# Another order for the first mixer: value projection, gates, state-space output and a half-and-half last projection

## The chip, the cores and the metric

The kernel runs on one core of one Trainium2 chip. Its time is the device time of one execution in microseconds (us); lower is better. The kernel before was timed in three executions. A fourth was recorded by the hardware profiler, and all rows below come from that one.

## The reference, cut to what matters

The program runs two blocks one after the other on a sequence of 256 tokens of width 1024, all in 32-bit floats. The first block is an adaptive-norm hybrid mixer followed by a mixture of 32 experts; the second block has its own mixer and experts and is not touched here. This is the part that the change is about (the linear recurrences are cut to their names):

```python
c_act = silu(c)
mod = (c_act @ ada_w + ada_b)                       # 6 vectors of 1024
sh1, sc1, g1, sh2, sc2, g2 = split(mod, 6)
h = rmsnorm(x, norm1_g) * (1 + sc1) + sh1
x = x + g1 * hybrid_mixer(h)
h = rmsnorm(x, norm2_g) * (1 + sc2) + sh2
x = x + g2 * moe_ffn(h)                             # top 4 of 32 experts

def hybrid_mixer(h):
    proj = h @ w_in                                 # 1024 x 6672: q,k,v | z | b,a | ssd_z | xbc | dt
    qkv = silu(causal_dwconv(gdn_qkv, w))           # convolution over 4 tokens
    q, k = l2norm(...), l2norm(...)                 # 8 heads of 128
    o = gated_delta_rule_chunked(q, k, v, beta, g)  # per chunk of 64 tokens a triangular
                                                    # inverse, then 4 chunks in sequence
    o = rmsnorm(o) * silu(z)
    xbc = silu(causal_dwconv(xbc, w) + b)
    y = ssd_chunked(...) * silu(ssd_z)              # state-space part, 16 heads of 64
    y = rmsnorm(y)
    return concatenate([o, y]) @ w_out              # 2048 x 1024
```

## The kernel before, in words

Weights come from memory in chunks of 1 MB (256 columns of 1024 rows, or 128 rows of 2048 columns of `ada_w`). All chunks, those of the experts too, go through one list that SP works off in order (`Stream`, line 173 issues each load). A load is issued when its slot is free: four slots while the mixer runs, six more ("ring 1") when the mixer has given back one side of its memory, and five at the mixer's end. So the next stage's loads queue up behind this stage's.

A projection is done in split precision: each weight chunk is turned into a high part `wh` (by ACT, line 296) and a rest `wl` (by DVE or POOL, line 293), one chunk ahead of its use, and `mm3` makes three matrix products of each pair (high by high, high by rest, rest by high). A chunk has two halves of 24 matmuls of 128x256 each; "half-chunk" below means these 24. All matmuls are issued at line 283, all plain ACT operations at line 296, all two-operand DVE operations at line 293.

The work of the first mixer is written as generators. `weave(main, (fill, rate))` takes one step of `main`, then `rate` steps of `fill`, and so on; a scheduler then places the instructions on their engines. `chain` runs generators one behind the other, `turns` in turns, `run_all` to the end. The stages, with the times of the profiled execution:

- **Stage A, 35 to 198 us.** Projection of `xbc` (6 chunks), `k` and `q` (8 chunks), each followed by `conv_silu`: ACT makes `cv_y`, DVE adds three shifted products (line 661), ACT takes a tanh (`cv_t`), DVE joins them to silu (line 664; silu(y) is y/2 times 1 + tanh(y/2), so the weights carry a factor 0.5). Beside it the state-space part `ssd()`, and the second third of the adaptive vector (`ada_batch(1)`): eight sums of 128x2048 on DVE (lines 477 and 479), then small matmuls.
- **Preparation, 198 to 291 us.** `gdn_prep`: decay matrices `dS`, `dT`, the products of keys, the triangular inverse by doubling. As fill at rate `FILL1` = 0.8: the state-space gate (4 chunks), then the values `v` (4 chunks) in turns with `ssd_cat`, which lays the gated state-space output out for the last projection. `ada_batch(2)` runs beside it at rate 0.25.
- **Recurrence, 291 to 363 us.** `gdn_steps`: four chunks of 64 tokens in sequence, each with two groups of heads; chunks 0 and 1 make token half 0 of `o`, chunks 2 and 3 half 1. As fill at rate `FILL2` = 0.6: the gate `z` (4 chunks), then `ssd_out` (the state-space half of the last projection, 4 chunks); what is left of the fill is run after it.
- **Tail, 363 to 411 us.** Ring 1 is opened; `o` is transposed (line 1126), multiplied by the gate and split; the other half of the last projection (4 chunks, both token halves) runs in split precision; behind each chunk `router_logits` adds the result to `x`, transposes it (line 1202) and multiplies it by the router weights.
- **Routing, 411 to 440 us.** The logits (line 1219), the choice of experts and their rows. The experts' biases `bsrc` (line 1627) are loaded by SP behind the 15 expert chunks. Then the experts run, 440 to 1340 us.

Of the kernel before, what the change touches and what calls it, by code (L numbers as in the profile page):

```python
# [24 lines left out]
KD = 8  # L25
# [92 lines left out]
class Stream:  # L118
# [57 lines left out]
    def get(self, split=False):  # L176
# [7 lines left out]
        return v  # L184

# [68 lines left out]
def chain(*gens):  # L254
    for g in gens:
        yield from g
# [13 lines left out]
def kernel_body(ctx, tc, ins, consts, out):  # L270
# [192 lines left out]
    def ada_batch(b):  # L463
# [4 lines left out]
        SP.dma_start(g, ada_b[0:1, 2048 * b + g0:2048 * b + g0 + 1024].to_broadcast([P, 1024]))  # L468
        acc = None
# [20 lines left out]
        ws.give(slot)  # L490

# [53 lines left out]
    nc.vector.tensor_scalar(col_w, pb[:, :144], 0.5, None, op0=ALU.mult)  # L545
    hb = pA.tile([P, 12], F32, name="hb")
    nc.vector.tensor_scalar(hb, colv("ssd_conv_b"), 0.5, None, op0=ALU.mult)
# [39 lines left out]
def mixer1(k):  # L587
# [4 lines left out]
    hT, h32, ro, col_w, hb, colv = k.hT, k.h32, k.ro, k.col_w, k.hb, k.colv  # L592
# [59 lines left out]
    def conv_silu(pj, wc, ct, nct, dst, bias=None):  # L652
# [44 lines left out]
    def twice_silu(pj):  # L697

        th = pA.tile([P, 512], F32, tag="t2a", bufs=2, name="hs")
        act(th, pj, AF.Tanh, scale=0.5)  # L700
        V.scalar_tensor_tensor(th, th, 1.0, pj, op0=ALU.add, op1=ALU.mult)
        return th

# [8 lines left out]
    def emit(c, pj):  # L712
        if c < 8:
            xT = pA.tile([P, T], F32, tag="vT", bufs=2, name="xT")
            conv_silu(pj, cws, c, 12, xT, bias=hb[:, c:c + 1])
# [4 lines left out]
        else:  # L720
            conv_silu(pj, cws, c, 12, bc[:, c - 8], bias=hb[:, c:c + 1])
# [236 lines left out]
    def ssd_gate():  # L958
        def emit(i, pj):
            g2 = twice_silu(pj)  # L960
# [8 lines left out]

        rsy = pA.tile([P, 4], F32, name="rsy")  # L970
        k.rstd(rsy, ssy, 0.25 / 512, pA, "rsy")
        for t in range(2):
            for g in range(2):
                y = ys[t][:, g * 512:(g + 1) * 512]
                V.tensor_scalar(y, y, rsy[:, t * 2 + g:t * 2 + g + 1], 0.5, op0=ALU.mult, op1=ALU.mult)
# [16 lines left out]
    def out_part(i, pj):  # L992
        sl = slice(i * 256, (i + 1) * 256)
        d = pA.tile([P, 2, 256], F32, tag="t2a", bufs=2, name="d")
# [18 lines left out]
    ada2 = k.ada_batch(2)  # L1013
# [5 lines left out]
    S = a4("S")  # L1019
    o = [a4(f"o{t}") for t in range(2)]  # L1020
# [12 lines left out]
    def gdn_steps():  # L1033
        for n in range(4):
# [33 lines left out]
            for hg in range(2):  # L1068
# [18 lines left out]
                if c == 1:  # L1087
                    gdn_norm(t, hg)
                yield
# [3 lines left out]
    def emit_z(i, pj):  # L1093
        if not zs:
            zs.extend(a4(f"zs{i}").rearrange("p (c s) -> p c s", c=4) for i in range(2))
        g2 = pA.tile([P, 512], F32, tag="zt", bufs=1, name="zt")
# [1451 lines left out]
```

## Time and profile before

| | us |
|---|---|
| three timed executions | 2166.81, 2175.94, 2178.86 |
| their median | 2175.94 |
| the profiled execution | 2167.87 |
| its span, first to last instruction | 2166.1 |
| of that, up to the end of the tail | 411 |
| routing | 411 to 440 |
| first experts | 440 to 1340 |
| second block | 1340 to 2166 |

PE is busy for 1929.7 us of the span (89%), DVE for 696.2 and ACT for 437.5. A share of the whole span says little here, since the stages differ: the first experts stand at the limit of the memory, while the first mixer has PE, DVE and ACT busy together. So the stretches of the mixer are to be read one by one. A busy PE is not a PE at its peak: its records lengthen when it waits for weights or runs at the lower of its two clock levels, and the granted clock stands beside each stretch.

### The profile page before, as it was taken

The numbers are of one execution on the slowest core, as the hardware profiler recorded it, in microseconds if no ns is written. First come the engines' busy times: TensorE is split into PE (matmuls) and PEld (weight loads), VectorE is DVE, ScalarE is ACT, GpSimd is POOL, SyncE is SP. The second block draws the span as 40 slices with busy tenths as digits, with TensorE's granted clock in tenths as the row PEclk, the third lists the DMA queues.
The fourth block names the chain that finished last, engine by engine and source line by source line (L and its number), as shares of the span: only waits on it lengthen the run. The fifth ranks groups of instructions, "written<-read, shape, count | busy, mean of one in ns | idle before, by whom it ended". The sixth has DMA issues, their size and how long they took to land. (4 is left out here: it accounts for less than half of the span.)

```text
span 2166.1 us, 27479 instructions
## 1 busy us (share of the span) xinstructions
PE 1929.7 (89%) x11276; PEld 1017.1 (47%) x11277; DVE 696.2 (32%) x1436; ACT 437.5 (20%) x1030; POOL 256.8 (12%) x206
## 2 busy tenths in 40 slices
PE   6889899589999999999999999889999688878777
PEld 3878788533343434334343433387779332212111
DVE  4888847421111211111111011464755200000001
ACT  3555434221010100001010100143443210101001
POOL 2524312100000000000000000243433000000000
PEclk8989889789999999999999999999999799999999
DMA  8553425679999999999999999925238699999997
GB/s 311 200 190 118 157 80 184 256 312 419 420 420 421 413 421 421 402 421 420 418 421 385 422 421 421 328 84 180 74 104 334 247 421 421 420 420 421 421 421 282
DMA packets 170747, 706.67 MB, mean 326 GB/s; under 512 B 20775, under 2 KB 83796, under 8 KB 95860
## 3 DMA queue, kind: packets, MB, share of 16 engines
q1 hardware_dynamic: 170612, 704.80, 82.0%
q8 instruction: 93, 1.52, 0.3%
q14 instruction: 42, 0.34, 0.0%
HBM read 703.70 MB, written 1.05 MB: 325 GB/s over the span
## 5 line engine op out<-in xcount | busy, mean ns | idle before, releaser
L283 PE MATMUL ps_gu<-w,xe 128*64 128x512 f32 (+1 forms) x3072 | 704.5, 630 | 66.2 <-DMA w<-in_w_up_dram 41.9
L283 PEld LDWEIGHTS ps_gu<-w,xe 128*64 128x64 f32 (+1 forms) x3072 | 226.9, 132 | 512.7 <-issue 377.6
L283 PE MATMUL ps_y<-w,aT 128*64 128x512 f32 (+1 forms) x1536 | 373.9, 600 | 14.6 <-DMA w<-in_w_down_dram 13.7
L283 PEld LDWEIGHTS ps_y<-w,aT 128*64 128x64 f32 (+1 forms) x1536 | 114.2, 127 | 235.6 <-issue 184.4
L293 POOL TENSOR_TENSOR wl<-w,wh 128x512 fp32r<-128x512 f32 x126 | 179.3, 1431 | 379.4 <-ACT wh L296 375.4
L1589 DVE TENSOR_SCALAR g<-ps_gu 128x512 f32<-128x512 f32 x32 | 22.0, 687 | 470.4 <-PE ps_gu L283 469.6
L296 ACT ACTIVATE wh<-w 128x512 fp32r<-128x512 f32 x244 | 139.4, 623 | 85.7 <-PE ps_pj L283 49.7
L283 PE MATMUL ps_pj<-hT,wh 128*128 128x256 f32 x704 | 147.0, 305 | 6.4 <-DVE cv_y L661 3.5
L293 DVE TENSOR_TENSOR wl<-w,wh 128x512 fp32r<-128x512 f32 x118 | 116.0, 1001 | 48.7 <-ACT wh L296 47.5
L283 PEld LDWEIGHTS ps_pj<-hT,wh 128*128 128x128 f32 x704 | 120.1, 207 | 12.1 <-issue 5.4
L293 DVE TENSOR_TENSOR x<-x,ps_g 128x512 f32<-128x512 f32 x96 | 66.0, 688 | 168.4 <-PE ps_g L283 168.4
L283 PE MATMUL ps_pj<-hT,wl 128*128 128x256 f32 x352 | 107.1, 304 | 5.0 <-DVE wl L293 2.5
L296 ACT ACTIVATE g<-g 128x512 f32<-128x512 f32 x32 | 20.1, 629 | 417.5 <-DVE g L1589 416.8
L283 PE MATMUL ps_g<-ys,sgT 128*128 128x512 f32 x192 | 93.6, 616 | 1.6 <-DVE ys L293 0.8
L293 DVE TENSOR_TENSOR a<-g,ps_gu 128x512 f32<-128x512 f32 x8 | 5.5, 688 | 257.4 <-PE ps_gu L283 257.4
L283 PE MATMUL ps_g<-sel,xo 128*128 128x256 f32 x320 | 77.8, 392 | 2.0 <-ACT xe L296 1.7
L296 ACT ACTIVATE xe<-ps_g,mcol,a 128x256 f32<-128x256 f32 (+1 forms) x72 | 38.1, 538 | 191.8 <-PE ps_gu L283 150.7
L283 PEld LDWEIGHTS ps_pj<-hT,wl 128*128 128x128 f32 x352 | 72.7, 207 | 6.9 <-DVE wl L293 2.8
L293 DVE TENSOR_TENSOR ys<-ps_y,gb 128x512 f32<-128x512 f32 x32 | 22.1, 692 | 159.4 <-PE ps_y L283 159.4
L283 PEld LDWEIGHTS ps_g<-sel,xo 128*128 128x128 f32 x320 | 56.0, 189 | 31.8 <-ACT xe L296 13.2
L283 PE MATMUL ps_pj<-uT,wh 128*128 128x256 f32 x384 | 70.2, 284 | 0.0
L283 PEld LDWEIGHTS ps_g<-ys,sgT 128*128 128x128 f32 x192 | 31.2, 188 | 64.1 <-issue 35.2
(535 smaller groups left out, 2114.0 us busy)
## 6 DMA issues: line engine op xcount, KB each, us to landing
w<-in_moe_w_gu_dram SPq DMA_DIRECT2D x256, 1024.0 KB
w<-in_moe_w_down_dram SPq DMA_DIRECT2D x120, 1024.0 KB
w<-in_w_gate_dram SPq DMA_DIRECT2D x64, 1024.0 KB
w<-in_w_up_dram SPq DMA_DIRECT2D x64, 1024.0 KB
w<-in_w_down_dram SPq DMA_DIRECT2D x64, 1024.0 KB
w<-in_w_in_dram SPq DMA_DIRECT2D x45, 1024.0 KB
w<-in_ada_w_dram SPq DMA_DIRECT2D x24, 1024.0 KB
w<-in_w_out_dram SPq DMA_DIRECT2D x12, 1024.0 KB
```

Of the source, the lines that this page charges most:

```text
L283: return nc.tensor.matmul(o, l, r, start=start, stop=stop)
L293: (eng or nc.vector).tensor_tensor(o, a, b, op=op)
L296: nc.scalar.activation(o, i, f, **kw)
L1589: V.tensor_scalar(g, gu[j], 7.0, None, op0=ALU.min)
```

## The change

It touches the first mixer alone. In the order of the program:

- silu is taken by ACT in one operation (`AF.Silu`). The DVE operation that joined tanh and value goes, at line 664 and for both gates, and with it the factors 0.5.
- `ada_batch(2)` is no longer summed on DVE: `ada_products` makes 32 matmuls of 128x512, a copy by ACT, four transposes and two broadcasts. `ada_batch(1)` keeps its sums.
- The fill has another order and one rate: `v`, the state-space gate, `ssd_cat`, `ssd_out`, `z`, and a new piece `first_tile`, all beside `gdn_prep` and `gdn_steps` together at `FILL1` = 0.88.
- The last projection of the recurrence's output is done by halves of the tokens. Half 0 (`gdn_cat(0)`, `gdn_out(0)`) stands in `first_tile`, beside the recurrence's last chunk; half 1 follows the recurrence. Its weights are not split: it runs as full 32-bit matmuls (8 of 128x256 for a chunk and a half), and its four weight chunks keep the four slots until half 1 has used them.
- The router's set-up moves from behind the recurrence into `first_tile`; `router_logits` takes one token half at a time.

```diff
-        th = pA.tile([P, T], F32, tag="cv_t", bufs=2, name="cv_t")
-        act(th, y, AF.Tanh)
-        V.scalar_tensor_tensor(dst, th, 1.0, y, op0=ALU.add, op1=ALU.mult)
+        act(dst, y, AF.Silu)
...
+    def ada_products(b, c0, g0, g):
+        pm = None
+        for kk in range(KD):
...
+            w = ws.get()
+            pm = pm or bank()
+            for j in range(4):
+                mm(pm[32 * j:32 * j + 32], cb[:, kk], w[:, j * 512:(j + 1) * 512], start=(kk == 0), stop=(kk == KD - 1))
+            ws.done()
+            yield
+        mr = pA.tile([P, 512], F32, tag="mr", name="mr")
+        act(mr, pm, AF.Copy)
...
-    fill = chain(ssd_gate(), turns(proj_ch(4, emit_v), ssd_cat()))
-    weave(gdn_prep(), (fill, FILL1), (ada2, RA[2]))
-    run_all(fill)
...
-    fill = chain(proj_ch(4, None, emit_z), ssd_out)
-    weave(gdn_steps(), (fill, FILL2), (ada2, RA[3]))
-    run_all(fill, ada2)
+    def gdn_cat(t):
+        for hg in range(2):
+            pt = bank()
+            for i in range(4):
+                h = hg * 4 + i
+                nc.tensor.transpose(pt[:, i * P:(i + 1) * P], o[t][:, h * P:(h + 1) * P], C("swap"))
+            sl = slice(t * P, (t + 1) * P)
+            V.scalar_tensor_tensor(catg[hg][:, :, sl], pt.rearrange("p (c s) -> p c s", c=4), gh, zs[hg][:, :, sl], op0=ALU.mult, op1=ALU.mult)
+
+    def gdn_out(t, emit):
+        for i in range(4):
+            if t == 0:
+                c = ws.raw()
...
+                held.append(c)
+            w, slot = held[i]
+            pj = bank("pj", PJ)
+            for kk in range(KD):
+                mm(pj[:, :256], catg[kk // 4][:, kk % 4, t * P:(t + 1) * P], w[:, kk * 256:(kk + 1) * 256], start=(kk == 0), stop=(kk == KD - 1))
+            if t:
+                ws.give(slot)
+            emit(i, t, pj[:, :256])
+            yield
+
+    def first_tile():
+        yield from ada2
+        r.extend(router())
+        while not done[0]:
+            yield
...
+        gdn_cat(0)
+        yield
+        yield from gdn_out(0, r[0].tile)
+
+    fill = chain(proj_ch(4, emit_v), ssd_gate(), turns(ssd_cat()), ssd_out, proj_ch(4, None, emit_z), first_tile())
+    weave(chain(gdn_prep(), gdn_steps()), (fill, FILL1), (ada2, RA[2]))
+    run_all(fill)
     pA.end(1)
...
     ws.ring(k.ring1, NR1, {"B": NR1})
...
-    for h in range(8):
-        pt = bank()
-        for t in range(2):
-            nc.tensor.transpose(pt[:, t * P:(t + 1) * P], o[t][:, h * P:(h + 1) * P], C("swap"))
-        cf = pA.tile([P, T], F32, tag="cf", bufs=2, name="cf")
-        V.scalar_tensor_tensor(cf, pt[:, :T], gh, zs[h // 4][:, h % 4], op0=ALU.mult, op1=ALU.mult)
-        split_into(cf, catg[h // 4][0][:, h % 4], catg[h // 4][1][:, h % 4])
...
-    run_all(proj_tok(4, lambda part, kk, t: catg[kk // 4][part][:, kk % 4, t * P:(t + 1) * P], emit))
-    logits(k.lg, k.cr)
+    gdn_cat(1)
+    run_all(gdn_out(1, r[0].tile))
+    r[1](k.lg, k.cr)
...
-FILL1 = 0.8
-FILL2 = 0.6
+FILL1 = 0.88
```

ACT at the start of the preparation, before. ACT_TABLE_LOAD brings in another table of functions; `ls` is a logarithm for the key and query lengths, `vec`, `dS` and `dT` are exponentials of the decays, `jk` a square.

```order
L296 ACTIVATE wh<-w 128x512
L296 ACT_TABLE_LOAD
L296 ACTIVATE ls<-ssq,c_64 128x32
L296 ACTIVATE jk_2046,ssy<-xs_333 128x512
L296 ACTIVATE jk_2049,ssy<-xs_334 128x512
L296 ACT_TABLE_LOAD
L296 ACTIVATE vec<-vec 128x64
L296 ACTIVATE dS<-dS 128x512 x2
L296 ACTIVATE dT<-dT 128x512 x2
L296 ACTIVATE hs<-ps_pj 128x512
```

The same place now; `vT<-cv_y` is the new silu of the values.

```order
L301 ACT_TABLE_LOAD
L301 ACTIVATE vT<-cv_y 128x256
L301 ACT_TABLE_LOAD
L301 ACTIVATE vec<-vec 128x64
L301 ACTIVATE cv_y<-ps_pj,col_w 128x256
L301 ACTIVATE wh<-w 128x512 x4
L301 ACTIVATE dS<-dS 128x512
L301 ACTIVATE vt_1878<-ps_g 128x128 x2
L301 ACTIVATE dS<-dS 128x512
L301 ACTIVATE vt_1879<-ps_g 128x128 x2
L301 ACT_TABLE_LOAD
L301 ACTIVATE vT<-cv_y 128x256 x2
```

Silu has a table of its own, and the silus of the values stand between the exponentials, so that a table load stands between them: from the start of the program to `vec` there are now 21 table loads where there were 5.

PE at the end of the recurrence, before: the recurrence's last products (`vn,dT`) stand between those of `ssd_out` (`wh,cs`), and the sums of `ada_batch(2)` (`c_64,w`) just ahead of them.

```order
L283 MATMUL ps_pj<-wh,cs_2368 128x256
L283 MATMUL ps_g<-c_64,w 128x1 x8
L283 MATMUL ps_g<-w,c_64 128x512 x2
L283 MATMUL ps_g<-vn,dT 64x128 x4
L283 MATMUL ps_pj<-wh,cs_2365 128x256
```

PE there now, from the middle of the recurrence's last chunk (`S,qk`) on: the products of the last projection's first half (`w,cg`) and its router part (`rw,xT`).

```order
L288 MATMUL ps_pj<-w,cg_4130 128x256 x4
L288 MATMUL ps_pj<-w,cg_4131 128x256 x4
L288 MATMUL ps_pj<-w,cg_4130 128x256 x3
L1254 MATMUL ps_g<-c_64,x 128x128 x2
L288 MATMUL ps_pj<-w,cg_4130 128x256
L288 MATMUL ps_pj<-w,cg_4131 128x256
L288 MATMUL ps_g<-rw,xT 128x32 x2
L288 MATMUL ps_g<-S,qk_844 64x128 x4
L288 MATMUL ps_g<-S,qk_845 64x128 x4
```

And further down on PE, the recurrence's last products and what follows them now.

```order
L288 MATMUL ps_g<-vn,dT 64x128 x3
L288 MATMUL ps_g<-rw,xT 128x32 x2
L288 MATMUL ps_g<-vn,dT 64x128 x5
L1147 MATMUL ps_g<-ca,o_3437 128x128 x4
L288 MATMUL ps_pj<-w,cg_4130 128x256 x2
L1147 MATMUL ps_g<-ca,o_3437 128x128 x4
```

Half 0 of the last projection now lies inside the last chunk of the recurrence, and only the transposes of half 1 (line 1147) and its 32 products come behind it; `ssd_out` stands far ahead.

SP, the sixth to the eleventh of the 15 loads of expert weights, with the engines' semaphores that each waits for, before.

```order
L173 DMA w_4318<-in_moe_w_gu_dram 128x2048 [waits DMAHW0_49]
L173 DMA w_4320<-in_moe_w_gu_dram 128x2048 [waits DMAHW1_49,Pool_49]
L173 DMA w_4409<-in_moe_w_gu_dram 128x2048 [waits DVE_49,DMAHW2_49,Activation_49,Pool_49]
L173 DMA w_4494<-in_moe_w_gu_dram 128x2048 [waits DMAHW3_49,DVE_49,Pool_49]
L173 DMA w_4579<-in_moe_w_gu_dram 128x2048 [waits DMAHW4_49,DVE_49,Pool_49]
L173 DMA w_4754<-in_moe_w_gu_dram 128x2048 [waits DMAHW5_49,DVE_49,PE_49]
```

The same six now.

```order
L173 DMA w_4357<-in_moe_w_gu_dram 128x2048 [waits DMAHW0_49]
L173 DMA w_4380<-in_moe_w_gu_dram 128x2048 [waits DMAHW1_49,PE_49]
L173 DMA w_4404<-in_moe_w_gu_dram 128x2048 [waits DMAHW2_49,PE_49]
L173 DMA w_4427<-in_moe_w_gu_dram 128x2048 [waits DMAHW3_49,PE_49]
L173 DMA w_4450<-in_moe_w_gu_dram 128x2048 [waits DMAHW4_49,PE_49]
L173 DMA w_4491<-in_moe_w_gu_dram 128x2048 [waits DMAHW5_49,DVE_49]
```

The four loads into the mixer's own slots waited for the splitting of the weights (ACT, DVE, POOL) and now wait for PE, which reads the unsplit chunks for half 1; the first six wait for ring 1 to open in both.

## Rows read from the trace of the kernel before

**Rows 1.** The page: busy share of the DMA engines in 40 slices.

```profile
DMA  8553425679999999999999999925238699999997
```

**Rows 2.** Busy time by stage: length, engines, granted PE clock, DMA share, GB/s.

```profile
35.00:198.00 163.00, 144.37 (x1005) 128.60 (x1005) 139.22 (x251) 91.21 (x254) 64.76 (x48) 0.91 0.55 182
198.00:291.00 93.00, 79.97 (x1851) 73.41 (x1852) 75.02 (x130) 38.81 (x92) 32.91 (x22) 0.92 0.47 149
291.00:363.00 72.00, 72.00 (x516) 61.02 (x516) 43.72 (x122) 29.36 (x85) 10.56 (x7) 0.88 0.31 101
363.00:411.00 48.00, 42.85 (x333) 40.34 (x332) 31.56 (x66) 16.08 (x40) 12.74 (x10) 0.96 0.63 244
411.00:440.00 29.00, 5.66 (x30) 4.82 (x29) 8.48 (x55) 5.07 (x11) 6.61 (x4) 0.54 0.55 203
440.00:1340.00 900.00, 885.98 (x3534) 351.38 (x3534) 149.01 (x275) 74.57 (x135) 2.64 (x3) 1.00 1.00 413
```

**Rows 3.** Busy time in two shorter stretches; columns PE, PEld, DVE, ACT, POOL.

```profile
80.00:140.00 60.00, 47.88 (x339) 43.13 (x340) 57.48 (x85) 32.98 (x92) 28.59 (x17) 0.89 0.66 220
291.00:310.00 19.00, 19.00 (x100) 14.42 (x99) 6.58 (x20) 3.85 (x11) 0.00 (x0) 0.74 0.01 1
```

**Rows 4.** Groups of DVE instructions in stage A: busy us, mean ns, idle before.

```profile
L661 DVE SCALAR_TENSOR_TENSOR cv_y<-ps_pj,col_w,cv_y 128x253 f32<-128x253 f32 (+2 forms) x84 | 37.3, 473 | 2.5 <-ACT cv_y L296 2.2
...
L479 DVE SCALAR_TENSOR_TENSOR w<-w,cact 128x2048 f32<-128x2048 f32 x7 | 16.4, 2341 | 0.0
...
L664 DVE SCALAR_TENSOR_TENSOR qk<-cv_t,cv_y 128x256 f32<-128x256 f32 x16 | 9.3, 587 | 1.3 <-ACT cv_t L296 1.1
...
L664 DVE SCALAR_TENSOR_TENSOR xT<-cv_t,cv_y 128x256 f32<-128x256 f32 x8 | 4.3, 542 | 1.4 <-ACT cv_t L296 1.4
L664 DVE SCALAR_TENSOR_TENSOR bc<-cv_t,cv_y 128x256 f32<-128x256 f32 x4 | 3.3, 843 | 0.0
```

**Rows 5.** Groups of DVE instructions in the preparation.

```profile
L479 DVE SCALAR_TENSOR_TENSOR w<-w,cact 128x2048 f32<-128x2048 f32 x5 | 12.3, 2453 | 0.7 <-DMA w<-in_ada_w_dram 0.5
...
L664 DVE SCALAR_TENSOR_TENSOR vT<-cv_t,cv_y 128x256 f32<-128x256 f32 x8 | 4.4, 550 | 2.7 <-ACT cv_t L296 2.6
```

**Rows 6.** ACT in order of time, around two table loads: start, duration, idle before.

```profile
192.09 1.28 ACT L296 ACT_TABLE_LOAD   x1
193.38 0.32 ACT L296 ACTIVATE ls<-ssq,c 128x32 f32<-128x32 f32 x1
...
195.15 1.28 ACT L296 ACT_TABLE_LOAD   x1
197.95 0.26 ACT L296 ACTIVATE vec<-vec 128x64 f32<-128x64 f32 x1 [1.52 <-DVE vec L843]
```

**Rows 7.** PE in order of time: three kinds of matmul, runs of like records joined.

```profile
30.28 1.06 PE L283 MATMUL ps_g<-w,cb 128*32 128x512 f32 x8 [2.85 <-DMA w<-in_ada_w_dram]
...
50.29 3.64 PE L283 MATMUL ps_g<-h,wsm 128*32 128x256 f32 x16
...
399.19 0.40 PE L283 MATMUL ps_pj<-wh,cg 128*128 128x256 f32 x2
...
399.55 0.40 PE L283 MATMUL ps_pj<-wh,cg 128*128 128x256 f32 x2
```

**Rows 8.** From the recurrence's last norm to the experts' first matmul, all engines.

```profile
362.06 0.31 ACT L296 ACTIVATE jk<-o 128x128 f32<-128x128 f32 x1
...
371.49 41.45 SPq L173 DMA_DIRECT2D w<-in_moe_w_gu_dram  x15
...
410.32 0.75 DVE L293 TENSOR_TENSOR x<-x,d 128x256 f32<-128x256 f32 x2
...
412.98 2.67 SPq L1627 DMA_DIRECT2D bsrc<-in_moe_b_gu_dram  x4
...
429.91 1.06 ACT L296 ACTIVATE bgu<-bsrc 128x1024 fp32r<-128x1024 f32 x1 [12.72 <-DMA bsrc<-in_moe_b_gu_dram]
...
439.96 1.98 PE L283 MATMUL ps_gu<-w,xe 128*64 128x512 f32 x4
```

More of the change, by code (lines that the diff above doesn't have):

```diff
@@ L184, in get, with raw @@
         return v
+    def raw(self):
+        self.fill()
+        return self._next("mm")
     def ready(self):
@@ L490, in ada_batch @@
         ws.give(slot)
+    def ada_products(b, c0, g0, g):
+        pm = None
+        for kk in range(KD):
+            while not ws.ready():
+                yield
[8 more added lines that the diff above has]
+        pt = bank()
+        for q in range(4):
+            nc.tensor.transpose(pt[:, q * P:(q + 1) * P], mr[:, q * P:(q + 1) * P], ident)
+        v = lambda a: a.rearrange("p (j q) -> p q j", j=2)
+        tt(v(mcol[:, 8 + 8 * b:16 + 8 * b]), pt.rearrange("p (q j r) -> p q j r", q=4, r=32)[:, :, c0 // 512:c0 // 512 + 2, 0],
+           v(colv("ada_b1")[:, 8 * b - 8:8 * b]), ALU.add)
+        for n in range(2):
+            r = 32 * (g0 // 512 + n)
+            pg = bank()
+            mm(pg, ident[:, r:r + 1].to_broadcast([P, P]), mr)
+            tt(g[:, n * 512:(n + 1) * 512], g[:, n * 512:(n + 1) * 512], pg, ALU.add)
     a0 = ada_first()
@@ L1033, in gdn_steps @@
     def gdn_steps():
+        S = a4("S")
+        o.extend(a4(f"o{t}") for t in range(2))
         for n in range(4):
@@ L1088, in gdn_steps @@
                     gdn_norm(t, hg)
+                    done[0] = hg == 1
                 yield
@@ L1101, in mixer1, with add, router @@
     k.spd = SPD[3]
-    fill = chain(proj_ch(4, None, emit_z), ssd_out)
-    weave(gdn_steps(), (fill, FILL2), (ada2, RA[3]))
-    run_all(fill, ada2)
+    gh = colv("gdn_norm_g")
+    catg, held = [], []
+    def add(t, sl, o):
+        d = pA.tile([P, 256], F32, tag="vT", bufs=2, name="d")
+        tt(d, o, gb[0][:, sl])
+        tt(x[:, t, sl], x[:, t, sl], d, ALU.add)
+    def router():
+        V.scalar_tensor_tensor(k.a2, k.mcol[:, 24:32], 1.0, colv("norm2_g"), op0=ALU.add, op1=ALU.mult)
+        pt = bank()
+        for kk in range(KD):
+            mm(pt[:, :32], k.mcol[:, 16 + kk:17 + kk].to_broadcast([P, P]), k.rw[:, kk], start=(kk == 0), stop=(kk == KD - 1))
+        tt(k.cr, pt[:, :32], k.rb, ALU.add)
+        tt(k.rw, k.rw, k.a2[:, :, None].to_broadcast([P, KD, 32]))
+        return router_logits(k, pA, add, lambda: pA.tile([P, 256], F32, tag="cf", bufs=2, name="xT"), k.rw, 32)
@@ new lines, in first_tile @@
+    def first_tile():
+        yield from ada2
+        r.extend(router())
+        while not done[0]:
+            yield
+        catg.extend(a4(f"cg{i}").rearrange("p (c s) -> p c s", c=4) for i in range(2))
+        gdn_cat(0)
+        yield
+        yield from gdn_out(0, r[0].tile)
+    r, done = [], [False]
+    ada2 = k.ada_batch(2)
+    fill = chain(proj_ch(4, emit_v), ssd_gate(), turns(ssd_cat()), ssd_out, proj_ch(4, None, emit_z), first_tile())
+    weave(chain(gdn_prep(), gdn_steps()), (fill, FILL1), (ada2, RA[2]))
```

104 lines of the change are left out of this document (46 added, 58 removed).

## Prediction

> **What bounds the kernel now.** I read the share of the memory engines over the span first, then the busy time stage by stage, and only then single groups. From the tenth slice on (a slice is 54 us) the memory engines stand at 9 or more tenths without a break until the second block's mixer [rows 1], and in the stretch of the first experts they are at 1.00 with 413 GB/s [rows 2]. Nothing that is done in the mixer makes the experts faster, but whatever brings their start forward brings the end forward by the same amount, since the list of loads behind it is one unbroken stream. So the question is when that start comes: 439.96 us now [rows 8].
>
> Back from there: the routing stretch 411 to 440 has PE busy 5.66 of 29 us [rows 2]. What ends last in it is a transfer: ACT waited 12.72 us for the experts' biases [rows 8], whose load was issued at 412.98 behind 15 loads of 1 MB. At 413 GB/s a load takes 1.05 MB / 413 = 2.5 us, so five of them that are issued when the tail ends are 12.7 us ahead of the biases. The start thus follows the end of the tail (x is complete at 410.32 + 0.75 = 411.1), plus any backlog of loads at that time.
>
> In the mixer three stretches have different limits. In stage A DVE is busy 139.22 of 163 us, and 57.48 of 60 us from 80 to 140 [rows 2, 3]; PE waits for it. In the preparation PE has 79.97 of 93 and DVE 75.02 [rows 2]: neither is full, a chain of small steps sets the pace. In the recurrence PE is busy all 72.00 us, but at a mean granted clock of 0.88, and in its first 19 us of 0.74, where almost no weights arrive (DMA share 0.01) and only 100 matmuls run [rows 2, 3]. The tail is 48.7 us (362.06 + 0.31 to 411.1), nearly all of it PE work in a row [rows 2, 8].
>
> **The change part by part.**
>
> *Stage A.* The join of tanh and value goes: 9.3 + 4.3 + 3.3 = 16.9 us of DVE over 28 pieces [rows 4]. The three shifted products of each piece (37.3 us) and the seven sums of the adaptive vector (16.4 us) stay. Where DVE is full, the saving comes off whole: 60 of 163 us, so 6.2 of the 16.9; of the other 10.7, in stretches where DVE is busy 81.7 of 103 us, I take a quarter, 2.7. Together **-9**. Against it stand table loads: the order has 16 more of them on ACT up to the exponentials, at 1.28 us each 20.5 us [rows 6]. I take them at nothing: ACT is busy 91.21 of 163 us [rows 2], so 112 with them, and the row of the second load shows one that is over 1.52 us before its operand is there. If that cover is gone, because silu is what PE or DVE waits for, all 20.5 come on top. Bounds: -17 (the whole saving) to +11.5 (-9 and all loads).
>
> The table loads are where a page speaks against this change. In the trace a load takes 1.28 us and the next operation starts at once: 192.09 + 1.28 = 193.37, and the logarithm starts at 193.38 [rows 6]. The Trainium skill, "ScalarE: Activation LUTs", section "What ACT_TABLE_LOAD costs", states about 1283 ns for the load and about 1380 ns of drain, 2.66 us for each switch, and its rules for authors ask to group operations by table set. By that price the 19 added switches of the mixer would be 50 us of ACT, an estimate from the page; the row shows the load's share and no drain behind it, so I keep 1.28.
>
> *Preparation.* DVE loses the five sums, 12.3 us, and eight joins, 4.4 us [rows 5]: 16.7. The products that take the sums' place are priced by the same kind of matmul at the program's start: the 8 records of one chunk took 1.06 us [rows 7], so six of the eight chunks that fall here are 6.4 us of PE. `ssd_out`, which came after the recurrence's middle, now lies here: at a spacing of three matmuls in 0.36 us (399.19 to 399.55 [rows 7]) a half-chunk of 24 is 2.84 us, four are 11.4. PE's gaps are 93 - 80 = 13.0 us. So 17.8 us of PE work meets 13 us of gaps, of which I let it use 8 (+9.8), and DVE's relief gives back half, 8.4. About **+1**. Three more table loads (3.8 us) stand among the exponentials and I hide them as in stage A. Bounds: -8 (the relief counts, all new PE work falls in gaps) to +12 (half the gaps, no relief).
>
> *Recurrence.* Fill before: about 13 half-chunks, 37 us. Fill after: 12 half-chunks (four of `ssd_out`, eight of `z`), 34 us, and half 0 of the last projection. Its 32 full 32-bit matmuls of 128x256 have a price in the trace: eight of this kind, recorded twice each, took 3.64 us [rows 7], so 0.455 us each and 14.6 us for 32. The router's set-up, its products and the rest of the adaptive vector are some 2 us more. -3 + 14.6 + 2 gives **+14**. Nothing hides it in a stretch where PE is busy without a gap; what could is the low clock at its start, where the fill now reaches without a break between the two weaves. Bounds: +5 (the stretch at clock 0.74 is filled and gives 19 x 0.26 = 5 us, and waits on DVE take up 4 more) to +20.
>
> *Tail.* Before, 48.7 us: what is left of `ssd_out`, transposes, splitting, 192 matmuls. After: norm of the last heads, eight transposes and gating (5 us), 32 x 0.455 = 14.6 us, 2 us for a clock not yet high, 1.5 for the last addition: 23. That is **-25**, bounded by -20 (each of the four pieces waits a us or so for its bank and its addition) and -27. No splitting stands in it: ACT, DVE and POOL are out of the way of PE.
>
> *What is queued behind.* On SP the experts' loads wait for slots. Six start when ring 1 opens, at the tail's beginning; the four into the mixer's slots now wait for PE in the last projection and come one by one in the tail; five follow at its end. Ten loads take 25 us and the tail has 23, less the opening: a backlog of one load stands before the last five and before the biases, **+2.5**. Ends: 0 and +5.
>
> Sum: -9 + 1 + 14 - 25 + 2.5 = -16.5. The profiled execution took 2167.87, so 2151.4; the median of the three is 8.1 us above the profiled one, which makes 2159.5, rounded to 2160.
>
> **The rivals.**
>
> *PE was full already.* The work of PE does not shrink: 64 matmuls in full precision cost 29 us where 192 split ones at 0.12 cost 23, and the adaptive products, 8 x 1.06, are 8.5 us more [rows 7]. If stage A is not held by DVE but by its own chain, and overlap only moves work, the recurrence grows by 20, the tail with its backlog shrinks by 22.5, and the rest is zero: -2.5, 2173.5. For it: PE busy 72.00 of 72 [rows 2]. Against it: DVE at 57.48 of 60 [rows 3]. Chance 0.20.
>
> *The table loads are exposed: slower.* Each silu stands in a chain (products, shifted sums, silu, transposes, the next piece's slot), and switching to its table and back puts 1.28 us into that chain each time. If all in stage A count and eat the relief too, A is +20.5; the preparation with its relief half gone +6; recurrence +14; tail -22.5: +18, or 2194. It decides from 16.5 / 1.28 = 13 exposed loads of the 19 on: beyond, the kernel is slower than before. For it: in the preparation DVE already waited 2.6 us for eight tanhs [rows 5], so ACT is not early there, and `cv_y` has only two buffers. Against it: in stage A DVE waited 1.1 + 1.4 us for 24 of them [rows 4], and ACT has 72 us free [rows 2]. Chance 0.12. By the page's 2.66 us for a switch it would decide from seven loads on; the row speaks against that price.
>
> *More than forecast.* The whole 16.9 us come off A, and v's projection beside the early preparation fills its gaps: -17, -3, recurrence +6 with its clock up, tail -22.5 without backlog: -36.5, 2139.5. For it: the low clock where no weights arrive [rows 3]. Chance 0.18.
>
> That the change does not do what it says, half 0 falling behind the recurrence, I can leave aside: in the order its products stand ahead of the recurrence's last ones.
>
> **How the numbers follow.** The forecast has 0.50, centred on 2160 and some 8 us wide to either side. 0.5% (11 us, about what a measurement of this kernel can tell from no change) puts the border at 2165: 0.37 of it is faster, 0.12 within, 0.01 slower. The third rival adds 0.18 faster; the first 0.03 faster, 0.16 within, 0.01 slower; the second 0.01 within, 0.11 slower. Sums: 0.58, 0.29, 0.13. The range goes from just below the third rival, 2137, to 2184, which takes in the first and half the way to the second.
>
> **What would show it.** In the profile after: stage A (up to the first exponentials) shorter by some 9 us with DVE less busy by 17; a table load on ACT followed at once by its operation, and no long wait of PE or DVE for a silu; PE busy throughout the recurrence, which is 14 us longer; from the last norm to the last addition to x some 23 us; biases landing some 21 us after that. The forecast is wrong if PE or DVE waits for ACT in stage A by more than 10 us, if the recurrence grows by 20 or more, or if the loads of the expert weights stand further back than one load at the tail's end.

## The result: slower, 2188 us where 2160 was forecast

| | before | after |
|---|---|---|
| median of 8 executions, us | 2174.93 | 2188.09 |
| lowest and highest | 2166.6, 2179.74 | 2178.85, 2192.44 |
| span of the profiled execution | 2166.1 | 2182.3 |

The ratio is 1.0065, interval 1.0042 to 1.0088: slower, since the whole interval lies above 1. The median is above the range's end of 2184. Relative to before that is some 13 us more where 16 less were forecast.

Five marks of the first mixer can be read from both traces, as start or end of one row each: the first exponential of the preparation (`vec<-vec`), the recurrence's first `vn`, the end of the last norm (`jk<-o`), the end of the last addition to x, and the experts' first matmul (`ps_gu<-w,xe`). All later texts use them.

| mark, us | before | after | step, forecast | step, measured |
|---|---|---|---|---|
| first exponential | 197.9 | 199.1 | -9 | +1.2 |
| recurrence begins | 289.5 | 295.3 | +1 | +4.6 |
| last norm ends | 362.5 | 392.1 | +14 | +23.8 |
| x complete | 411.1 | 414.6 | -25 | -26.0 |
| experts begin | 440.0 | 449.7 | +2.5 | +6.2 |
| sum | | | -16.5 | +9.8 |

The first experts' last load is issued 9.9 us later too (1375.9 and 1385.8), so the shift is carried through them one to one, as forecast. The other 6.3 us of the two profiles (spans 2166.1 and 2182.3) arise in the second block's mixer, whose instructions stand in the same order in both. From that load to the first load of its experts' weights it took 245.8 us before and 252.0 after; all runs below but one (the run with one table, at a clock of 0.63) took between 245.7 and 254.6 us, so this part is taken for chance.

**By stage.** Columns as in [rows 2]:

```profile
35.00:199.00 164.00, 146.59 (x1020) 129.74 (x1021) 128.31 (x227) 112.28 (x269) 63.29 (x41) 0.95 0.57 188
199.00:295.00 96.00, 84.84 (x1874) 71.73 (x1872) 52.04 (x112) 41.41 (x94) 25.02 (x22) 0.91 0.41 134
295.00:392.00 97.00, 92.60 (x715) 80.79 (x712) 49.07 (x132) 33.72 (x97) 11.64 (x9) 0.98 0.27 88
392.00:415.00 23.00, 19.41 (x92) 16.29 (x92) 8.48 (x29) 2.39 (x10) 0.30 (x1) 0.85 0.88 353
415.00:450.00 35.00, 4.98 (x24) 4.34 (x24) 9.34 (x59) 6.05 (x11) 5.41 (x3) 0.56 0.63 236
```

Stage A and the preparation lost 10.9 and 23 us of DVE work, and neither became shorter, although stage A's granted clock was 0.95 where it had been 0.91 [rows 2]. The recurrence has 715 matmuls where it had 516 [rows 2], at nearly full clock.

**DVE and ACT in stage A** (35 to 199 us), groups as in [rows 4]:

```profile
L697 DVE SCALAR_TENSOR_TENSOR cv_y<-ps_pj,col_w,cv_y 128x253 f32<-128x253 f32 (+2 forms) x92 | 40.6, 472 | 9.3 <-ACT cv_y L301 8.7
L298 DVE TENSOR_TENSOR wl<-w,wh 128x512 fp32r<-128x512 f32 x37 | 36.3, 1001 | 6.7 <-ACT wh L301 6.5 <-issue 0.2
...
L301 ACT ACT_TABLE_LOAD x20 | 25.7, 1283 | 2.2 <-DVE cv_y L697 1.9
```

The last of these loads and the operation behind it, in order of time:

```profile
197.83 1.28 ACT L301 ACT_TABLE_LOAD   x1
199.12 0.26 ACT L301 ACTIVATE vec<-vec 128x64 f32<-128x64 f32 x1
```

The second group's row in the trace before was this:

```profile
L293 DVE TENSOR_TENSOR wl<-w,wh 128x512 fp32r<-128x512 f32 x34 | 32.9, 977 | 2.9 <-ACT wh L296 2.0 <-issue 0.9
```

DVE waits 8.7 us for ACT's `cv_y` where it waited 2.2 [rows 4], and 6.5 for ACT's `wh` where it waited 2.0. ACT has twenty table loads in it, 25.7 us. And there are 92 shifted sums instead of 84: with the values first in the fill, their first convolutions fall into this stage.

**PE's fill in the recurrence**, before (290 to 362.4 us) and then after (295.3 to 392.1), with one group of the recurrence's own matmuls (`vn,dT`): busy us and mean ns.

```profile
L283 PE MATMUL ps_pj<-hT,wh 128*128 128x256 f32 x80 | 17.9, 313 | 0.0
L283 PE MATMUL ps_pj<-wh,cs 128*128 128x256 f32 x79 | 15.1, 286 | 0.0
L283 PE MATMUL ps_pj<-hT,wl 128*128 128x256 f32 x40 | 11.9, 297 | 0.0
L283 PE MATMUL ps_g<-vn,dT 64*64 64x128 f32 x64 | 11.3, 331 | 0.0
L283 PE MATMUL ps_pj<-wl,cs 128*128 128x256 f32 x39 | 10.9, 279 | 0.0
```

```profile
L288 PE MATMUL ps_pj<-hT,wh 128*128 128x256 f32 x128 | 24.4, 289 | 0.0
L288 PE MATMUL ps_pj<-hT,wl 128*128 128x256 f32 x64 | 18.0, 282 | 0.0
L288 PE MATMUL ps_pj<-w,cg 128*128 128x256 f32 x64 | 15.5, 388 | 0.0
L288 PE MATMUL ps_pj<-wh,cs 128*128 128x256 f32 x80 | 15.5, 286 | 0.0
L288 PE MATMUL ps_pj<-wl,cs 128*128 128x256 f32 x40 | 11.2, 279 | 0.0
L288 PE MATMUL ps_g<-vn,dT 64*64 64x128 f32 x64 | 8.7, 276 | 0.0
```

Before, 80 + 79 + 40 + 39 = 238 split matmuls lay beside the recurrence; after, 128 + 64 + 80 + 40 = 312, and the 32 full ones of half 0 (64 records, 15.5 us). The recurrence's own matmuls became shorter at the higher clock (`vn,dT` from 331 to 276 ns).

**Behind the recurrence**, PE in order of time, after:

```profile
387.44 1.30 PE L288 MATMUL ps_g<-vn,dT 64*64 64x128 f32 x10
393.57 1.09 PE L1147 MATMUL ps_g<-ca,o 128*128 128x128 f32 x4 [4.83 <-DVE rs_q L402]
395.61 2.07 PE L288 MATMUL ps_pj<-w,cg 128*128 128x256 f32 x4 [0.95 <-DVE cg L1149]
397.48 1.06 PE L1147 MATMUL ps_g<-ca,o 128*128 128x128 f32 x4
398.33 4.54 PE L288 MATMUL ps_pj<-w,cg 128*128 128x256 f32 x19
```

PE stands still for 4.83 and 0.95 us while the last norm and gating run (3.3 of the 4.83 lie ahead of the norm's end). The four matmuls behind take 2.07 us, at a granted clock of 0.50; four at full clock take 1.03.

**Loads and the experts' start**, after; they answer to [rows 8]:

```profile
392.08 24.37 SPq L173 DMA_DIRECT2D w<-in_moe_w_gu_dram  x15
416.53 7.76 SPq L1685 DMA_DIRECT2D bsrc<-in_moe_b_gu_dram  x4
...
426.47 0.32 SPq L1783 DMA_DIRECT2D sb<-in_g_mix_dram  x1
...
439.69 1.06 ACT L301 ACTIVATE bgu<-bsrc 128x1024 fp32r<-128x1024 f32 x1 [19.57 <-DMA bsrc<-in_moe_b_gu_dram]
...
445.88 1.28 ACT L301 ACT_TABLE_LOAD   x1 [5.14 <-POOL bgu L298]
...
449.74 1.12 PE L288 MATMUL ps_gu<-w,xe 128*64 128x512 f32 x2
```

The first of the 15 loads now starts 20.6 us later than in [rows 8], and all 15 come in one heap of 24.4 us. The biases are read 25.1 us after x is complete; before it was 18.8. The chain in this kernel runs from the biases over POOL to ACT's next table and the first matmul; `sb` is the first of the second block's small loads, which SP issues in between. What SP's loads waited for from 391 to 420 us (total us, times, longest):

```profile
SPq L173 <- PE ps_pj L288: 13.2, 4, 3.7
SPq L173 <- DVE o L298: 4.3, 1, 4.3
```

The second load of the heap goes out only at 396.8, when DVE is done with `o`, and four wait for PE's products of half 1.

### The profile page after: what moved, and what is told of

Its sections match the earlier page's. It is cut to its first block, busy times and chain, and to the rows that moved or that the text cites. A ratio compares the mean times of both kernels' runs of the same rounds, so it can differ in the third digit from the quotient of the medians.

```text
span 2182.3 us, 27327 instructions
## 1 busy us (share of the span) xinstructions
PE 1939.0 (89%) x11264; PEld 1017.9 (47%) x11265; DVE 643.8 (30%) x1369; ACT 452.5 (21%) x1027; POOL 234.3 (11%) x191
## 5 line engine op out<-in xcount | busy, mean ns | idle before, releaser
L288 PE MATMUL ps_y<-w,aT 128*64 128x512 f32 (+1 forms) x1536 | 370.0, 601 | 14.8 <-DMA w<-in_w_down_dram 12.8
L298 POOL TENSOR_TENSOR wl<-w,wh 128x512 fp32r<-128x512 f32 x111 | 158.4, 1434 | 305.6 <-ACT wh L301 283.5
L288 PE MATMUL ps_pj<-hT,wh 128*128 128x256 f32 x704 | 141.7, 296 | 9.5 <-DVE cv_y L697 4.2
L301 ACT ACTIVATE wh<-w 128x512 fp32r<-128x512 f32 x228 | 129.2, 622 | 84.5 <-PE ps_pj L288 45.0
L288 PEld LDWEIGHTS ps_pj<-hT,wh 128*128 128x128 f32 x704 | 114.3, 196 | 17.3 <-issue 5.3
L288 PEld LDWEIGHTS ps_pj<-uT,wh 128*128 128x128 f32 x384 | 60.8, 195 | 4.2 <-issue 3.7
```

The costliest lines, as they stand in the source:

```text
L288: return nc.tensor.matmul(o, l, r, start=start, stop=stop)
L298: (eng or nc.vector).tensor_tensor(o, a, b, op=op)
L301: nc.scalar.activation(o, i, f, **kw)
```

## The experiments

Three theories. **PE**: the first mixer as a whole is bound by PE's work, so that relief of DVE and overlap buy nothing, and new PE work costs its price. **Table loads**: ACT's switches hold it up. **Heap**: the experts' start follows the loads, which start later. The forecast's own view, that DVE bounds stage A and overlap pays, is the fourth.

Marks come from one profiled execution of each kernel, and they scatter with the granted clock. By how much is told by four traces whose mixer is the changed kernel's own: the changed kernel itself (x complete at 414.6), the same again (420.1), and two runs below whose edits lie behind the mixer, the biases ahead (414.5) and fewer loads ahead of the loop (428.6). A mark of x inside 414.5 to 428.6 therefore tells nothing; the medians of the timed executions weigh more. Runs without an interval were executed once.

**Sums again for the last third of the adaptive vector.**

```diff
-        if b == 1:
-            yield from ada_sums(b, c0, g0, g)
-        else:
-            yield from ada_products(b, c0, g0, g)
+        yield from ada_sums(b, c0, g0, g)
```

> The changed kernel with one part undone: the last third of the adaptive vector is summed on DVE again instead of by PE products. PE theory (the first mixer is bound by PE throughout, and the products are 17 us of new PE time against 5 that they replace): the recurrence's last norm comes 8 to 12 us earlier than 392, the experts start as much earlier than 449.7, time 2176 to 2180. Table-load theory (ACT's switches hold the mixer up): DVE gets 19 us of work back, PE's relief is idle time, within 3 us of the changed kernel, 2185 to 2191.

Median 2180.79, ratio to before 1.0013 (0.9991 to 1.0035), against 1.0065 (1.0042 to 1.0088) for the changed kernel: the two intervals do not meet, so the products do cost time. The marks do not show it: x complete 415.4, experts' start 449.8. But its first exponential came at 205.3 in a stage A at clock 0.90, in which the edit changes nothing. A second trace of this kernel is below.

**Tanh and joins again.**

```diff
-        act(dst, y, AF.Silu)
+        th = pA.tile([P, T], F32, tag="cv_t", bufs=2, name="cv_t")
+        act(th, y, AF.Tanh)
+        V.scalar_tensor_tensor(dst, th, 1.0, y, op0=ALU.add, op1=ALU.mult)
```

> The changed kernel with silu made from a tanh and a joining DVE operation again, in the convolution and in both gates; 19 table loads of 1.28 us go, some 22 us of DVE work return. Table-load theory: the exponentials at the end of stage A come 10 us or more earlier than 199.1, time below 2178. PE theory: stage A holds the same PE work, the exponentials stay within 3 us of 199.1, time 2185 to 2191.

Median 2184.16, ratio 1.0047 (1.0022 to 1.0073): within noise of the changed kernel. The first exponential came at 194.2, 4.9 us earlier, so the loads do cost stage A more than the joins did; but x was complete at 419.8, inside the scatter of the changed kernel's. Each theory was half right, and the mixer's end did not gain.

**Half 0 behind the recurrence.**

```diff
     def first_tile():
         yield from ada2
         r.extend(router())
-        while not done[0]:
-            yield
...
-        yield from gdn_out(0, r[0].tile)
...
+    gdn_cat(0)
+    run_all(gdn_out(0, r[0].tile))
     gdn_cat(1)
     run_all(gdn_out(1, r[0].tile))
```

> The changed kernel with token half 0 of the last projection done behind the recurrence, ahead of half 1, and no longer beside it. PE theory: the 15 us only change their place; last norm about 376 instead of 392, x complete at 414 plus or minus 4; ring 1 opens 15 us earlier, so that the loads are less in a heap and the experts start 443 to 450. The forecast's view (the overlap itself pays, since the recurrence has room): x complete 10 to 15 us later, at 425 to 430, experts' start at 455 or later, time 2195 or more.

Median 2171.10, ratio 0.9998 (0.9972 to 1.0024), an interval that does not meet the changed kernel's: the loss is gone. Last norm 374.9, x complete 409.9, experts' start 440.4, all as the PE theory had it or earlier. Two more kernels with half 0 behind, below, have x complete at 407.9 and 413.0, so all three lie ahead of the changed kernel's 414.5 to 428.6. PE at the same place as above:

```profile
370.99 1.08 PE L288 MATMUL ps_g<-vn,dT 64*64 64x128 f32 x8 [0.35 <-ACT vn L301]
372.00 1.09 PE L1147 MATMUL ps_g<-ca,o 128*128 128x128 f32 x8
373.57 5.01 PE L288 MATMUL ps_pj<-w,cg 128*128 128x256 f32 x22 [0.48 <-DVE cg L1149]
```

Half 0 now does what it could not do inside the recurrence: it keeps PE at work while the last norm runs, with a wait of 0.48 us instead of 4.83 + 0.95, and the clock stays up (1.00 from 375 to 410 us, where the tail above had 0.85). The loads start 17 us earlier as well.

**Biases ahead of the last five chunks.**

```diff
+    k.bsrc = pB.tile([P, 1024], F32, tag="a", name="bsrc")
+    for i in range(4):
+        nc.sync.dma_start(k.bsrc[32 * i:32 * i + 32], ...)
     ws.ring(pB, N2 - NR1, {"B": N2 - NR1})
```

> The changed kernel with the experts' biases loaded ahead of the last five of the 15 expert chunks. If the experts' start only waits for the biases, it comes at x complete (414.6) plus some 13 us of routing, 428 to 431, 20 us earlier, and the time is 2168 to 2172. If the program's loop ahead of the experts waits for every load that is under way, the start follows the last of the 15 loads (some 436): 438 to 442, 8 to 12 us earlier, time 2176 to 2181.

Median 2172.96, ratio 0.9995 (0.9977 to 1.0013); start at 443.1, 6.6 us earlier, with x complete at the same 414.5.

```profile
424.11 1.06 ACT L301 ACTIVATE bgu<-bsrc 128x1024 fp32r<-128x1024 f32 x1 [4.12 <-DMA bsrc<-in_moe_b_gu_dram]
425.31 4.74 POOL L298 TENSOR_TENSOR bgu<-bsrc,bgu 32x1024 fp32r<-32x1024 f32 x2 [9.70 <-ACTq L1542]
439.23 1.28 ACT L301 ACT_TABLE_LOAD   x1 [14.06 <-SPq L1542]
...
442.47 0.34 SPq L1784 DMA_DIRECT2D sb<-in_g_mix_dram  x1
...
443.09 1.12 PE L288 MATMUL ps_gu<-w,xe 128*64 128x512 f32 x2
```

SP's own waits at that line (400 to 450 us), and two stretches with the columns of [rows 2]:

```profile
SPq L1542 <- SPq L1542: 14.2, 5, 4.6
...
430.00:436.00 6.00, 0.00 (x0) 0.00 (x0) 0.00 (x0) 0.00 (x0) 0.05 (x1) 0.50 0.95 393
436.00:443.00 7.00, 1.91 (x8) 1.78 (x8) 1.44 (x7) 2.25 (x3) 0.00 (x0) 0.50 0.06 22
```

The biases are done at 430, and ACT, which read them at 424.11, waits 14.06 us for SP at line 1542. That line is the loop for overfull experts that stands ahead of the experts. SP waits there five times, 14.2 us in all, as long as the memory engines are busy (DMA share 0.95 up to 436 us, 0.06 behind). Four more runs below with the biases ahead show the same: a DMA share of 0.44 to 0.70 while SP waits there, 0.01 to 0.04 behind its last wait. From this it is read that SP passes the loop only when its outstanding loads have landed. So the second hypothesis holds for this kernel: the start follows the last of the 15 loads (443.1; 438 to 442 had been expected). The gain of 6.6 us is not the biases' alone, since the second block's small loads, which went out ahead of the loop from 426.47 on, now follow it, from 442.47 on.

**Two products of three in the fill.** `proj_ch` without an emitter for channels (gate z) and `proj_tok` (state-space gate and output) leave out the product of the activations' low part.

```diff
-        mm(o, l[0], r[0], start=start, stop=False)
-        mm(o, l[0], r[1], start=False, stop=False)
-        mm(o, l[1], r[0], start=False, stop=stop)
+        mm(o, w[0], r[0], start=start, stop=False)
+        mm(o, w[1], r[0], start=False, stop=stop)
```

> The changed kernel without the product of the activations' low part in four projections: state-space gate, gate z and the state-space half of the last projection take two products of three, 192 matmuls of about 0.12 us less (22.7 us of PE), nothing else is changed; part of the computation is left out. PE theory: x is complete 15 to 23 us earlier than 414.6. Chain theory (PE is kept busy, but the steps of inverse and recurrence and the clock set the pace): less than 8 us earlier.

```profile
397.65 0.42 DVE L298 TENSOR_TENSOR x<-x,d 128x256 f32<-128x256 f32 x1
```

x complete at 398.1, 16.5 us earlier than in the changed kernel's first trace, and ahead of its whole scatter. Of these, 2.9 us had come before the first exponential (196.25), where the edit changes nothing; so of 22.7 us of PE work taken away, 60 to 73% came off the end, with the work of DVE and ACT nearly unchanged (236.5 and 188.5 us busy from 35 us to x complete, 237.9 and 189.8 without the edit). That is the PE theory. The one execution took 2171.18 us.

**One shifted sum of three left.**

```diff
-        for s in (1, 2, 3):
+        for s in (1,):
```

> The changed kernel with one of the three shifted sums of each convolution piece, so that 88 DVE operations of about 0.47 us go (some 41 us, two thirds of it in stage A); part of the computation is left out. If DVE bounds stage A, as the forecast had it, the exponentials come 10 us or more earlier than 199.1 and x is complete 10 us or more earlier than 414.6. If PE bounds it, both move by 4 us or less.

The edit takes away two sums of three, not one: 108 become 36 in the mixer, 51.0 us of DVE become 17.1. In stage A that is 26.8 us, about the two thirds of 41 that were expected. The convolution loses taps here, so the experts are chosen otherwise, and only the mixer's marks can be compared.

```profile
186.33 0.26 ACT L301 ACTIVATE vec<-vec 128x64 f32<-128x64 f32 x1
...
409.55 0.43 DVE L298 TENSOR_TENSOR x<-x,d 128x256 f32<-128x256 f32 x1
```

The sums that are left in stage A (35 to 186.3 us), as the first group above:

```profile
L697 DVE SCALAR_TENSOR_TENSOR cv_y<-ps_pj,col_w,cv_y 128x255 f32<-128x255 f32 x29 | 13.8, 475 | 17.9 <-ACT cv_y L301 17.9
```

The first exponential came 12.8 us earlier, so DVE does take part in setting when stage A ends, though 14 of the 26.8 us were lost: DVE's wait for ACT's `cv_y` grew from 8.7 to 17.9 us. But x was complete only 4.6 us earlier, so that each theory is right at one of the two marks, or nearly. What DVE gives back in stage A is mostly not time at the end: PE's work, less of which then lies in stage A (976 matmuls instead of 1020), has to be done later.

**Fewer loads ahead of the loop**, with the biases ahead:

```diff
-    ws.ring(pB, N2 - NR1, {"B": N2 - NR1})
...
     m.rest(rounds_of(k, pool, sel, 64), Load1(k, pool, ins))
+    ws.ring(pool, N2 - NR1, {"B": N2 - NR1})
```

> The changed kernel with the biases loaded ahead and the last five expert chunks listed behind the loop that precedes the experts, so that 12 loads instead of 15 stand ahead of it. Loop theory (the start waits for every load under way): 12 loads land at some 427, the experts start at 431 to 435 instead of 449.7 (biases ahead alone: 443.1), time 2160 to 2167. If the start hangs on the biases alone, it stays at 443.

> Half 0 behind the recurrence and the loads as in the run with 12 loads ahead of the loop. The two gains add: x complete at 410, experts' start 426 to 432 instead of 440.4, time 2158 to 2164, faster than the kernel before by 0.5% or more. If they share one cause, the start is no earlier than 435.

Medians 2175.14, ratio 1.0007 (0.9974 to 1.0040), and 2173.90, ratio 1.0003 (0.9971 to 1.0034): both above what was expected and not told from the same kernels with the biases ahead alone. The starts, 451.8 and 434.9, missed too. From x complete to the start the first took 23.1 us, against 28.6 with the biases ahead alone. The second took 26.9, against 25.2 with half 0 behind and the biases ahead (below): there the edit brought nothing. The reason stands in both traces: the eleventh and twelfth loads went out late, just ahead of the loop (438.7 and 439.1, and 421.4 and 421.8), and SP then waits at the loop's line twice. In the first:

```profile
SPq L1541 <- SPq L1541: 7.4, 2, 4.9
```

So loads under way hold the loop, but listing five of them later did not pay. The trace of the first ran stage A at a low clock:

```profile
35.00:208.00 173.00, 155.66 (x1016) 137.97 (x1017) 129.14 (x227) 112.38 (x269) 61.05 (x41) 0.88 0.54 178
```

That is the same stage as in the table by stage above, 1016 matmuls against 1020, 9 us longer at 0.88 instead of 0.95.

**One table for all of the mixer.**

> The changed kernel with a tanh where silu stands in the first mixer, as one ACT operation and nothing added on DVE: the same number of operations everywhere, but no table switch between the convolutions and the exponentials; another function is computed, so what follows the mixer is not comparable. Table-load theory: the exponentials come 8 to 13 us earlier than 199.1 and x is complete 8 us or more earlier than 414.6. PE theory: the exponentials come earlier by what DVE waited longer for ACT (5 to 11 us), but x only by 0 to 5.

```profile
35.00:190.00 155.00, 151.24 (x821) 136.28 (x822) 108.61 (x185) 75.83 (x211) 58.34 (x38) 0.63 0.51 169
```

A granted clock of 0.63 where the others had 0.88 to 0.96: this run tells nothing of the table loads.

**The biases ahead in the kernel before, half 0 behind with the biases ahead, and that with the sums.**

> The kernel before with the biases loaded ahead of the last five expert chunks and nothing else. If the start follows the last of the 15 loads: 431 to 435 instead of 440, time 2165 to 2170. If the biases alone hold it: 425 to 429, time 2160.

> The changed kernel with half 0 of the last projection behind the recurrence and the biases ahead of the last five chunks. x complete at 408 to 412, start 430 to 434 (440.4 without the biases), time 2161 to 2167.

> As the run with half 0 behind and the biases ahead, and the last third of the adaptive vector by sums on DVE. PE theory: at an equal granted clock 8 to 11 us of PE go, x complete 400 to 404, time 2153 to 2160. If the products only fill PE's gaps: x and time as without, within 3 us.

| | median, us | ratio to before | x complete | experts begin |
|---|---|---|---|---|
| before, biases ahead | 2167.31 | 0.9973 (0.9946 to 1.0000) | 409.9 | 432.8 |
| half 0 behind, biases ahead | 2165.22 | 0.9966 (0.9944 to 0.9988) | 413.0 | 438.2 |
| the same with sums | 2161.73 | 0.9958 (0.9939 to 0.9977) | 402.1 | 426.7 |

With the biases ahead the kernel before starts its experts at 432.8, as the loop theory had it. With half 0 behind, x and the start came later than expected (413.0 and 438.2, against 408 to 412 and 430 to 434). The last kernel is faster than the one before by 0.4%; its median is just above the expected 2153 to 2160. But its interval overlaps that of the kernel before with the biases ahead, so apart from the biases' place nothing here is shown to gain on the kernel before. By the marks the sums are worth 6 to 11 us of the mixer here (402.1 against 407.9, 409.9 and 413.0 in the three runs with half 0 behind and products), at nearly equal clock (0.94 against 0.95 from 35 us to x complete); by the medians 3.5 us, which is not told from nothing.

**Four last runs**: the changed kernel and the run with sums once more, the best kernel with tanh, and the changed kernel with the state-space gate ahead of the values.

```diff
-    fill = chain(proj_ch(4, emit_v), ssd_gate(), ...
+    fill = chain(ssd_gate(), proj_ch(4, emit_v), ...
```

> The changed kernel itself, a second look. If the differences between runs with the same stage A (exponentials at 198.9, 199.1, 205.3, 208.3; granted clock 0.95, 0.95, 0.90, 0.88) are the clock's, the exponentials come at 199 with a clock of 0.95 or later with a lower one, about 1.7 us for each 0.01; x complete between 414 and 424. If they come from the edits of those runs, it repeats 199.1 and 414.6 within 0.5.

> The run with sums instead of products in the changed kernel, a second look. PE theory: at a clock of 0.95 in stage A x is complete at 404 to 408 and the experts start at 439 to 443; the first look's 415.4 was its clock of 0.90. If the products cost nothing there, x is again at 414 to 416 with a clock of 0.95.

> The run with half 0 behind, the biases ahead and the sums (2161.7), with tanh and joins again instead of silu. Table-load theory: the loads cost stage A more than the joins, x complete 4 us or more earlier than 402.1, time 2153 to 2158. PE theory: within 3 us of 402.1, time 2158 to 2165.

> The changed kernel with the fill in the order of before: the state-space gate first, then the values. The values' convolutions leave stage A (92 shifted sums there instead of 84): the exponentials come 2 to 6 us earlier than 199.1 at an equal clock; by the PE theory x is complete within 3 us of 414.6; if the order of the fill had cost the time, x is complete 6 us or more earlier.

| | first exponential | x complete | experts begin | time |
|---|---|---|---|---|
| changed kernel again | 201.6 | 420.1 | 454.9 | 2187.26, one run |
| sums again | 201.8 | 413.9 | 447.2 | 2174.34, one run |
| best with tanh | 197.2 | 401.1 | 425.7 | 2160.15, ratio 0.9960 (0.9940 to 0.9980) |
| gate first | 203.7 | 417.4 | 450.6 | 2180.95, one run |

The changed kernel's own marks move by 5.5 us at x between its two traces (clock 0.95 and 0.93 in stage A). The sums once more had x at 413.9 with a clock of 0.94, where the PE theory wanted 404 to 408. Silu against tanh shows no difference in the best kernel's time. Gate first, the exponentials did not come earlier, against what was expected, though stage A's clock was 0.91 in this trace, and x stayed within the scatter of the changed kernel: nothing here makes the order of the fill the cause.

What stays open: how much the sums are worth. Inside the changed kernel the medians give 7 us and the marks of x no clear gain (413.9 and 415.4, against 414.5 to 428.6); with half 0 behind the marks give 6 to 11 us and the medians 3.5. Not tested by themselves were the fill's rate of 0.88 and the last projection in full precision, whose 64 matmuls the prediction prices 6 us above the 192 split ones.

## Why the prediction was wrong, point by point

**What bounds the mixer: the step that failed first.** DVE was read as the bound of stage A, from 57.48 of 60 us [rows 3], and its relief was booked as time at the end, -9. The run with one shift shows that less DVE work does bring stage A's end forward, but of its 12.8 us only 4.6 reach x; the run with two products shows that of 22.7 us of PE's work 13.6 to 16.5 do. Fill flows across the stage borders: a stage that ends earlier holds less fill, and the next one gets it. Both runs were executed once. The first rival (PE was full already) comes nearest with its "overlap only moves work"; that DVE has no part in stage A's length is not borne out. It was still 12.3 us short: preparation 4.6, recurrence 3.8, tail with backlog 2.7, stage A 1.2.

**Stage A, +1.2 instead of -9: the table loads, booked at nothing.** Of the 16.9 us of joins DVE's busy time kept 10.9 as gain, among other things because eight shifted sums of the values moved in; and its waits for ACT grew from 2.2 + 2.0 to 8.7 + 6.5 us, 11.0 together, under twenty table loads. With tanh and joins instead, the first exponential came 4.9 us earlier in the changed kernel (199.1 to 194.2) and 2.7 in the best one (199.9 to 197.2), so in stage A the loads cost more than the joins had. At the end of the program this does not show: neither of the two runs with tanh was told from its partner by its time.

The Trainium skill, "ScalarE: Activation LUTs", section "What ACT_TABLE_LOAD costs", has a switch at 2.66 us with its drain. Here twenty loads take 25.7 us, 1283 ns each, with 2.2 us of idle time ahead of all twenty, 1.9 of it for DVE; and behind the load at 197.83 the exponential starts at once (197.83 + 1.28 = 199.11, 199.12). No run here shows a drain.

**Preparation, +4.6 instead of +1.** It took up part of `ssd_out` and of the adaptive products, and its 23 us of DVE relief did not shorten it. What each part of the 3.6 us was worth was not measured.

**Recurrence, +23.8 instead of +14: the fill was mis-sized.** The term for the fill before was counted from the list of steps (13 half-chunks) and not from the trace, which has 238 split matmuls there, 9.9 half-chunks. After, 312 of them, 13 half-chunks where 12 were booked: so the fill grew by 74 x 0.12 = 9 us and was booked at -3. These 12 us are the largest error, and the terms that the sum left out offset each other in part: PE stood idle for 4.5 of the 96.8 us (none before), while the higher clock (0.98 instead of 0.88) shortened the recurrence's own matmuls. Half 0's 32 matmuls cost 15.5 us against 14.6.

**Tail, -26.0 against -25: right**, with the full matmuls at their price. But its gain was bought: with half 0 behind the recurrence the tail was 35 us and x all the same complete 4.7 us earlier (1.6 to 6.7 in the three traces). The overlap as such was worth less than nothing, since it took away the only work that could cover the last norm.

**Backlog, +6.2 instead of +2.5: mis-sized.** That the biases stand behind the loads was rightly read, and the step is theirs: 25.1 us behind x instead of 18.8. One load of backlog was foreseen. But the second load went out only at 396.8, and nine loads of 2.5 us from there end at 419.3, an estimate, 4.7 us behind x. What was not seen is the wait behind this one: with the biases ahead, the loop that waits for the loads under way still held the start at 443.1, where the biases alone would have let it come at 428 to 431.

**Adaptive products, booked as 6.4 us in the preparation's gaps.** Their price was about right (in all, 64 records of 128x512 from 35 to 392 us are busy 9.6 us, against 8.5 by the price); that gaps would hide them was not: going back to sums gave 7 us of the changed kernel's median.

The prediction's own three signs of being wrong all came: more than 10 us of waiting for ACT in stage A (15.2), a recurrence longer by 20 or more (23.8), and loads further back than one load (6.2 us).

## What to carry to other kernels

Where a fill flows freely beside a chain of stages, a stage's own bound says when the stage ends, not when the program does: leave out a known piece of one engine's work, once per engine, and see what reaches the end. Work that is independent of a serial tail is best kept to cover it; drawn forward into a stretch where its engine has no gaps, it only leaves the tail bare. Count the work that lies beside a stage in the trace and not in the program's list of steps. And before pricing a transfer, look for the loop or barrier behind it that waits for everything that is under way.

## What was not expected of the hardware

The same stage A, in kernels whose edits lie behind it, ran at granted clocks of 0.95, 0.93, 0.90 and 0.88 and took from 164 to 173 us (first exponential 198.9 to 208.3). Clock and time go together only roughly: at 0.93 the first exponential came at 199.9, 201.6 and 203.4. So a single trace of this mixer can be off by 9 us at the first exponential and by 14 at x (414.5 to 428.6). One run with other data had 0.63. While SP waits for its loads ahead of the experts, PE's clock is at its lower level (0.50 from 420 us to the experts' start) in the traces of before, of after and of the run with the biases ahead, so the experts begin on it. And between a table load and the operation behind it ACT loses nothing that the rows show (1283 ns for the load, the operation at once), where the operand is there.
